# Moving the attention-gate projections of a hybrid attention / SSM layer from the merge into the attention rounds

## The chip, the cores and the metric

The program runs on one core of one Trainium2 chip. The metric is the device time of one execution in microseconds. The kernel before took 1139.73 us (median of 3 runs, 1139.62 to 1141.38).

## The reference

One decoder layer over a sequence of 512 positions with 1024 channels, float32, and a last RMSNorm. Cut to what matters here:

```python
h = rmsnorm(x, norm_mix)
q, c_raw, q_idx, k_idx, w_idx, z, xbc, dt_raw, g_att, g_ssm = split(h @ w_in)
# A: sparse attention, 16 heads over a shared latent, k = 128 keys per query
att   = per-head softmax(q_lat . c_sel * scale + bias) @ c_sel, up-projected by w_uv
y_att = att @ w_att_out
# B: Mamba-2 SSD branch on z, xbc, dt
y_ssm = gated_group_rmsnorm(ssd(...), z) @ w_ssm_out
merged = sigmoid(g_att) * y_att + sigmoid(g_ssm) * y_ssm
x = x + merged @ w_out
h = rmsnorm(x, norm_ffn)
x = x + (silu(gate) * val) @ w_ffn_down      # gate, val: conv3(h @ w_ffn_up)
out = rmsnorm(x, norm_final)
```

g_att and g_ssm are two products of h with 1024 x 1024 pieces of w_in. The kernel writes sigmoid(g) as (tanh(g / 2) + 1) / 2.

## The kernel before

Every matrix product is done in three passes: an operand is split into a rounded high part and the rest (hi, lo), and hi x hi, hi x lo and lo x hi are added up in PSUM (`mm3`, L108; in groups that can be interleaved with other work, `proj_steps`, L373). A projection of 128 output channels over all 512 positions is 24 matmuls of 512 columns. Weights come in tiles of 128 x 1024: `fetch` (L91) loads one into `wr` (2 buffers) through SyncE's queue; `halves` (L101) makes `wh` on ScalarE (L86) and `wl` on GpSimd (L87), 3 buffers each. PSUM has two rings of four tiles, `mm` (projections) and `ch` (all else).

The stages in order: the first norm (`norm_T`, L126, called at L200), which squares and scales four blocks of x (lines L137 to L144), transposes them on TensorE (L146) and splits the result into hTh and hTl (L151, L152), which start in pairs as PSUM comes free; small projections (pkidx, pcr, pqidx); the top-k scores; the SSD branch by four groups; the attention; the merge; the output projection; the FFN; the last norm.

The attention is a loop of 18 rounds (L854). Round h computes the logits of head h (pl, L767, read with the bias and the running maximum by VectorE at L769), softmax (exponentials on ScalarE at L776, reciprocal and four scalings of 128, 256, 384 and 512 columns on VectorE, L778 to L781), the transposes of head h-1's probabilities (pPT, L797), and the product of head h-2's probabilities with V (pav, L816). `weave` (L359) puts fill between these: in even rounds the next query projection (pq, then pk), in odd ones a projection of the SSM gate (pgs, `gs_steps`, L736). Ahead of the rounds stand the first two query projections and the last SSD output projection (pso, L481). The bias rows T are loaded per head (L748).

The merge (L889) does, for each of 8 blocks of 128 channels: the attention-gate projection pga, its tanh (L893), the attention's output projection pao (L896), their product, the sum with the SSM part (L897, L898), and the split into mg.

A framework schedules the written program: it places each instruction on its engine by a model of the engines' times, keeping what depends on what, so the order on an engine differs from the order of the code by small steps. At run time each engine follows its own order and waits at semaphores. SyncE's queue issues the DMAs in its order too: one that waits holds those behind it.

Of the kernel before, what the change touches and what calls it, by code (L numbers as in the profile page):

```python
# [9 lines left out]
F32 = mybir.dt.float32  # L10
R32 = mybir.dt.float32r
AF = mybir.ActivationFunctionType
OP = mybir.AluOpType

P = 128
S = 512
NB = S // P
D = 1024
KD = D // P
# [29 lines left out]
def _body(ctx, tc, x, prm_d, cst_d, nfin_d, wI_d, wX_d, wSO_d, wQ_d, wG_d, wAO_d, wO_d, wUp_d, wDn_d,  # L49
          wkv_d, out):  # L50
    nc = tc.nc
# [10 lines left out]
    def mmt(name):  # L62
        return pm.tile([P, 512], F32, tag="mm", name=name)

    def cht(name):
        return pc.tile([P, 512], F32, tag="ch", name=name)
# [17 lines left out]
    def split(hi, lo, src, lo_eng=None):  # L84

        nc.scalar.activation(hi, src, AF.Copy)  # L86
        (lo_eng or nc.vector).tensor_tensor(lo, src, f(hi), OP.subtract)  # L87
# [10 lines left out]
    def weight(src, w=1024):  # L98
        return halves(fetch(src, w), w)

    def halves(fetched, w=1024):  # L101
        i, raw = fetched
        hi = wp.tile([P, w], R32, tag="wh", name=f"wh{i}", bufs=3)
        lo = wp.tile([P, w], R32, tag="wl", name=f"wl{i}", bufs=3)
        split(hi, lo, raw, lo_eng=nc.gpsimd)
        return hi, lo

    def mm3(ps, terms):  # L108
# [50 lines left out]
    def proj_T(ps, w):  # L159
        mm3(ps, [((w[0][:, k * P:(k + 1) * P], w[1][:, k * P:(k + 1) * P]), actT[k]) for k in range(KD)])  # L160
# [22 lines left out]
    with tc.tile_pool(name="n1", bufs=2) as n1:  # L183
# [13 lines left out]
        w1 = fetch(wI_d[1])  # L197
        nc.sync.dma_start(prm, prm_d)
        nc.sync.dma_start(cs1, cst_d[:, NKEEP:])
        norm_T(xts, "gmix", actT, n1, "vvaa", "aavv")  # L200
        w0, w1 = halves(w0), halves(w1)


        ps = mmt("pkidx")
# [168 lines left out]
    def proj_steps(name, wsrc, after, parts=2):  # L373

        st = {}

        def seq():
            wh, wl = st["w"]
            for a, b in ((wh, 0), (wh, 1), (wl, 0)):
                for k in range(KD):  # L380
                    yield a[:, k * P:(k + 1) * P], actT[k][b]

        def part(j):
            def run():
                if j == 0:
                    st["w"] = weight(wsrc)
                    st["ps"] = mmt(name)
                    st["it"] = list(seq())
                for i in range(24 * j // parts, 24 * (j + 1) // parts):
                    nc.tensor.matmul(st["ps"], *st["it"][i], start=(i == 0), stop=(i == 23))  # L390
                if j == parts - 1:
                    after(st["ps"])
            return run

        return [part(j) for j in range(parts)]
# [320 lines left out]
    def q_steps(p):  # L716
        def after(ps):
            qTs[p] = dup_q(ps, f"qT{p}", ("qh0", "ql0", "qh1", "ql1"), ap_, 0.125, 2)

        def k_step():  # L720
            ps = mmt(f"pk{p}")
            ks = slice(p * P, (p + 1) * P)
            mm3(ps, [((wkv[0][0][:, ks], wkv[0][1][:, ks]), ckvT)])
            kl = ap_.tile([P, S], R32, tag="tmp", name=f"kl{p}", bufs=1)
            kTs[p] = []
            for hh in range(2):
                r, o = slice(64 * hh, 64 * hh + 64), slice(64 - 64 * hh, 128 - 64 * hh)
                kt = ap_.tile([P, S], R32, tag=f"kT{hh}", name=f"kT{p}_{hh}")
                nc.scalar.activation(kt[r], ps[r], AF.Copy)
                nc.vector.tensor_tensor(kl[r], ps[r], f(kt[r]), OP.subtract)  # L730
                nc.sync.dma_start(f(kt[o]), f(kl[r]))
                kTs[p].append(kt)

        return proj_steps(f"pq{p}", wQ_d[p], after, 4) + [k_step]

    def gs_steps(p):  # L736
        def after(ps):
            tg = ap_.tile([P, S], F32, tag="tmp", name=f"tgs{p}", bufs=1)
            nc.scalar.activation(tg, ps, AF.Tanh, scale=0.5)
            nc.vector.scalar_tensor_tensor(yssm[p], tg, 1.0, yssm[p], OP.add, OP.mult)  # L740
        return proj_steps(f"pgs{p}", wG_d[8 + p], after, 4)

    def logits(h):
        p, hh = h // 2, h % 2
        qh, ql = qTs[p][hh]
        kt = kTs[p][hh]
        T = ap_.tile([P, 256], F32, tag="T", name=f"T{h}")
        nc.sync.dma_start(T, bass.AP(tensor=skD.tensor, offset=skD.offset + h * P * UW + 127,  # L748
                                     ap=[[UW - 1, P], [1, 256]]))
        bm = ap_.tile([P, SEGW], F32, tag="bm", name=f"bm{h}", bufs=1)  # L750
        r31 = pv("r31", h, h + 1)
        nc.gpsimd.tensor_tensor(bm[:, 0:P], msk[:, 0:P], T[:, P:], OP.add)
        nc.gpsimd.tensor_tensor(
            bass.AP(tensor=bm.tensor, offset=bm.offset + P, ap=[bm.ap[0], [512, 3], [1, 256]]),
            bass.AP(tensor=msk.tensor, offset=msk.offset + P, ap=[msk.ap[0], [512, 3], [1, 256]]),
            T.unsqueeze(1).to_broadcast([P, 3, 256]), OP.add)
        for i in (2, 3):
            o, n = SEG[i], (i - 1) * P
            nc.gpsimd.tensor_tensor(bm[:, o:o + n], msk[:, o:o + n], r31.to_broadcast([P, n]), OP.add)
        pr = ap_.tile([P, SEGW], F32, tag="pr", name=f"pr{h}")  # L760
        mx = ap_.tile([P, NB], F32, tag="mx", name=f"mx{h}")
        sm = ap_.tile([P, NB], F32, tag="sm", name=f"sm{h}")

        def lg(i):
            o, n = SEG[i], (i + 1) * P
            pl_ = cht(f"pl{h}_{i}")[:, :n]
            nc.tensor.matmul(pl_, qh[:, i * P:(i + 1) * P], kt[:, :n], start=True, stop=False)  # L767
            nc.tensor.matmul(pl_, ql[:, i * P:(i + 1) * P], kt[:, :n], start=False, stop=True)
            nc.vector.tensor_tensor_reduce(pr[:, o:o + n], pl_, bm[:, o:o + n], 1.0, -3e38, OP.add, OP.max,  # L769
                                           mx[:, i:i + 1])  # L770

        def soft():
            nc.vector.tensor_scalar(mx, mx, -1.0, None, OP.mult)  # L773
            for i in range(NB):
                o, n = SEG[i], (i + 1) * P
                nc.scalar.activation(pr[:, o:o + n], pr[:, o:o + n], AF.Exp, bias=mx[:, i:i + 1],  # L776
                                     accum_out=sm[:, i:i + 1])
            nc.vector.reciprocal(sm, sm)  # L778
            for i in range(NB):
                o, n = SEG[i], (i + 1) * P  # L780
                nc.vector.tensor_scalar(pr[:, o:o + n], pr[:, o:o + n], sm[:, i:i + 1], None, OP.mult)  # L781
            prs[h] = pr

        return [lambda i=i: lg(i) for i in range(NB)] + [soft]
# [57 lines left out]
    last_trans()  # L842
    for s_ in qn[1][:-1]:
        s_()
    so[0]()
    so[1]()
    load_kv()
# [3 lines left out]
    so[4]()  # L851
    so[5]()
    qn[1][-1]()
    for h in range(H + 2):  # L854
        p = h // 2
        fl = []
        if h == 2:
            open_att()
        if h < 2:
            hg = len(gs[0]) // 2  # L860
            fl = [so[6 + h]] + gs[0][h * hg:(h + 1) * hg]
        elif h < H:
            if h % 2 == 0 and p + 1 < 8:
                fl = list(qn[p + 1])
            elif h % 2 == 1:
                fl = list(gs[p])
        chain = []
        lg = logits(h) if h < H else []
        chain += [(i < 3, s_) for i, s_ in enumerate(lg[:NB])]
        if h >= 2:  # L870
            chain.append((0, lambda: pav_(h - 2)))
        if 1 <= h <= H:
            chain += [(i == 1, s_) for i, s_ in enumerate(ptrans(h - 1))]
        if h % 4 == 1 and h < H:
            chain.append((0, v_step(h // 4)))
        chain += [(1, s_) for s_ in lg[NB:]]
        if h >= 5 and h % 2 == 1:
            chain.append((0, lambda: att_split((h - 5) // 2)))
        weave(chain, fl)
# [7 lines left out]
    mp = mps.enter_context(tc.tile_pool(name="mp", bufs=1))  # L887
    mg = []
    for d in range(KD):  # L889
        ps = mmt(f"pga{d}")  # L890
        proj_T(ps, weight(wG_d[d]))
        tg = mp.tile([P, S], F32, tag="tg", name=f"tga{d}", bufs=2)
        nc.scalar.activation(tg, ps, AF.Tanh, scale=0.5)  # L893
        ps = cht(f"pao{d}")
        wh, wl = weight(wAO_d[d])
        mm3(ps, [((wh[:, k * P:(k + 1) * P], wl[:, k * P:(k + 1) * P]), attT[k]) for k in range(KD)])  # L896
        nc.vector.scalar_tensor_tensor(tg, tg, 1.0, ps, OP.add, OP.mult)  # L897
        nc.vector.tensor_tensor(tg, tg, yssm[d], OP.add)  # L898
        hi = mp.tile([P, S], R32, tag=f"mh{d}", name=f"mh{d}", bufs=1)
        lo = mp.tile([P, S], R32, tag=f"ml{d}", name=f"ml{d}", bufs=1)  # L900
        split(hi, lo, tg)
        mg.append((hi, lo))
# [207 lines left out]
```

## Time and profile before

| | us |
|---|---|
| median of 3 runs | 1139.73 |
| the profiled execution | 1139.14 |
| its span, first to last instruction | 1137.4 |
| TensorE matmul busy | 1092.4 (96%) |
| VectorE, ScalarE, GpSimd busy | 670.8, 588.5, 504.6 |
| attention, from the first query projection to pao's first | 429 to 637 |
| merge, up to the output projection | 637 to 719 |

The busy time of TensorE is modelled from overlapping matmuls, so the throughput is read from the distance of many matmuls in the chain, and the holes from the time that an engine sat idle before an instruction. Idle time of an engine off the chain costs nothing. The granted clock is a share of 2.4 GHz; the lower of the two levels, 1.2 GHz, is 0.5.

### The profile page before, as it was taken

What the parts mean: (1) busy time and instruction counts of PE and PEld (TensorE: products, weight loads), DVE (VectorE), ACT (ScalarE), POOL (GpSimd) and SP (SyncE); (2) the same over time, 40 slices, a digit from 0 to 9 for tenths busy, and PEclk for the clock granted to TensorE, in tenths of its full rate; (3) what the DMA queues carried; (4) which work ended last, traced back from release to release, by engine and by line L of the source; (5) the groups of instructions that cost most, each with busy time, mean ns of one, the idle gap of its engine ahead of it and who ended that gap; (6) DMA issues with size and microseconds to landing.
All of it is one profiled execution on the core that took longest, in us unless ns stands there. A gap on an engine that the chain in (4) does not pass through costs nothing.

```text
span 1137.4 us, 14581 instructions
## 1 busy us (share of the span) xinstructions
PE 1092.4 (96%) x5268; PEld 908.3 (80%) x5268; DVE 670.8 (59%) x1340; ACT 588.5 (52%) x948; POOL 504.6 (44%) x279
## 2 busy tenths in 40 slices
PE   5999999999999999899998999999999999999997
PEld 5777778788888887787887888878888888888885
DVE  4589999995696894588889433135344343420004
ACT  5364686687777744467666432244444444431223
POOL 3424244345344345656665344443444444444442
PEclk9999999999999999999999999999999999999999
DMA  5464332323332324334433233323322232222322
GB/s 195 117 190 146 111 103 84 105 93 108 102 97 90 130 73 117 127 88 121 130 88 101 86 130 111 112 85 103 109 93 93 97 106 93 93 93 95 106 96 74
DMA packets 43305, 122.06 MB, mean 107 GB/s; under 512 B 5392, under 2 KB 9760, under 8 KB 43232
## 3 DMA queue, kind: packets, MB, share of 16 engines
q1 hardware_dynamic: 42656, 120.07, 33.6%
q10 hardware_dynamic: 576, 1.05, 0.2%
q8 instruction: 42, 0.69, 0.2%
q14 instruction: 31, 0.25, 0.1%
HBM read 108.29 MB, written 5.32 MB: 100 GB/s over the span
## 4 chain that ended last, share of the span: by engine, by line
PE 65%; DVE 19%; ACT 4%; POOL 3%; issue 3%; DMA 1%; POOLq 0%; DVEq 0%; ACTq 0%
PE pup L112 21%; PE pdn L971 10%; PE pxbc L390 6%; PE pso L481 5%; PE pao L112 4%; PE pga L112 4%; PE pwo L915 4%; DVE msk L350 2%; DVE m L349 2%; DVE u L405 2%; DVE pr L781 2%; DVE pr L769 2%; PE pz L456 1%; PE pz L457 1%; PE pz L458 1%
## 5 line engine op out<-in xcount | busy, mean ns | idle before, releaser
L87 POOL TENSOR_TENSOR wl<-wr,wh 128x1024 fp32r<-128x1024 f32 x168 | 406.0, 2417 | 504.3 <-ACT wh L86 250.3
L86 ACT ACTIVATE wh<-wr 128x1024 fp32r<-128x1024 f32 x168 | 177.9, 1060 | 216.7 <-PE pdn L971 80.6
L954 DVE SCALAR_TENSOR_TENSOR fu<-pup,prm,fu 128x511 f32<-128x511 f32 x88 | 65.9, 749 | 124.5 <-ACT fu L952 122.9
L112 PE MATMUL pup<-hTh,wh 128*128 128x512 f32 (+1 forms) x368 | 88.0, 381 | 1.6 <-ACT hTh L151 0.8
L112 PE MATMUL pup<-hTl,wh 128*128 128x512 f32 (+1 forms) x368 | 87.7, 380 | 0.0
L112 PE MATMUL pup<-hTh,wl 128*128 128x512 f32 (+1 forms) x368 | 87.5, 380 | 0.0
L112 PEld LDWEIGHTS pup<-hTh,wh 128*128 128x128 f32 x368 | 67.2, 188 | 15.1 <-ACT hTh L151 1.0
L112 PEld LDWEIGHTS pup<-hTl,wh 128*128 128x128 f32 x368 | 67.3, 188 | 13.1
L112 PEld LDWEIGHTS pup<-hTh,wl 128*128 128x128 f32 x368 | 67.2, 188 | 13.1
L971 PE MATMUL pdn<-wl,fh 128*128 128x512 f32 x176 | 68.6, 390 | 1.2 <-POOL wl L87 1.2
L971 PE MATMUL pdn<-wh,fl 128*128 128x512 f32 x176 | 68.5, 389 | 0.0
L971 PE MATMUL pdn<-wh,fh 128*128 128x512 f32 x176 | 68.4, 390 | 0.0
L998 DVE TENSOR_TENSOR x<-pdn,x 128x512 f32<-128x512 f32 x8 | 5.5, 689 | 104.6 <-PE pdn L971 104.6
L405 DVE SCALAR_TENSOR_TENSOR u<-pxbc,prm,u 128x511 f32<-128x511 f32 (+2 forms) x72 | 53.3, 740 | 8.5 <-ACT u L403 8.3
L456 PE MATMUL pz<-wh,hTh 128*128 128x512 f32 x128 | 51.8, 405 | 1.1 <-DVE u L405 1.1
L390 PE MATMUL pxbc<-hTl,wh 128*128 128x512 f32 x192 | 52.0, 393 | 0.0
L390 PE MATMUL pxbc<-hTh,wh 128*128 128x512 f32 x192 | 51.4, 395 | 0.0
L457 PE MATMUL pz<-wl,hTh 128*128 128x512 f32 x128 | 50.8, 396 | 0.0
L458 PE MATMUL pz<-wh,hTl 128*128 128x512 f32 x128 | 50.7, 396 | 0.0
L390 PE MATMUL pxbc<-hTh,wl 128*128 128x512 f32 x192 | 50.4, 392 | 0.0
L952 ACT ACTIVATE fu<-pup,prm 128x512 f32<-128x512 f32 x44 | 34.3, 780 | 27.4 <-PE pup L112 27.4
L776 ACT ACTIVATE pr<-pr,mx 128x128 f32<-128x128 f32 (+1 forms) x64 | 35.5, 556 | 14.5 <-DVE mx L773 14.5
(361 smaller groups left out, 2514.2 us busy)
## 6 DMA issues: line engine op xcount, KB each, us to landing
wr<-wUp SPq DMA_DIRECT2D x44, 512.0 KB, 3.5
wr<-wX SPq DMA_DIRECT2D x40, 512.0 KB, 3.5
wr<-wDn SPq DMA_DIRECT2D x22, 512.0 KB, 3.4
dec<-acD SPq DMA_DIRECT2D x32, 256.0 KB, 3.8
wr<-wSO SPq DMA_DIRECT2D x16, 512.0 KB, 3.5
wr<-wG SPq DMA_DIRECT2D x16, 512.0 KB, 3.7
x<-x SPq DMA_DIRECT2D x8, 512.0 KB, 4.5
wr<-wQ SPq DMA_DIRECT2D x8, 512.0 KB, 3.5
```

What stands on the lines that cost most here:

```text
L86: nc.scalar.activation(hi, src, AF.Copy)
L87: (lo_eng or nc.vector).tensor_tensor(lo, src, f(hi), OP.subtract)
L112: nc.tensor.matmul(ps, l, r, start=(i == 0), stop=(i == len(seq) - 1))
L390: nc.tensor.matmul(st["ps"], *st["it"][i], start=(i == 0), stop=(i == 23))
L405: nc.vector.scalar_tensor_tensor(u[:, d:], ps[:, :S - d], pv("cw", o + 3 - d, o + 4 - d), u[:, d:], OP.mult, OP.add)
L456: nc.tensor.matmul(ps, actT[k][0][:, bs], wh[:, ws], start=(k == 0), stop=False)
L457: nc.tensor.matmul(ps, actT[k][0][:, bs], wl[:, ws], start=False, stop=False)
L458: nc.tensor.matmul(ps, actT[k][1][:, bs], wh[:, ws], start=False, stop=(k == KD - 1))
L481: nc.tensor.matmul(ps, *seq[i], start=(i == 0), stop=(i == 11))
L915: nc.tensor.matmul(po8[b][hf], l[:, bs], r[:, ws], start=(k == 0 and i == 0), stop=(k == KD - 1 and i == 2))
L954: nc.vector.scalar_tensor_tensor(u[:, d:], ps[:, :S - d], pv("fw", o + 2 - d, o + 3 - d), u[:, d:], OP.mult, OP.add)
L971: nc.tensor.matmul(po8[b][hf], l[:, bs], r[:, ws], start=(k == 0 and i == 0), stop=(k == NF - 1 and i == 2))
```

## The change

Four things change.

The attention-gate projections (pga) leave the merge. `ga_steps(d)` builds each as four groups of six matmuls, like those of pgs; their tanh is written to a DRAM tile gaD. The first of the eight runs ahead of pso, the other 28 groups are dealt to the 18 rounds by `GA_SHARE` and mixed into each round's fill. The merge loads the tanh back (tile tg, four buffers), and its pao takes PSUM tiles from both rings in turn.

The tile kl / tgs / tga has two buffers instead of one, and the bias rows T have one instead of two.

The scalings of 384 and 512 probabilities go from VectorE to ScalarE.

In the first norm, ScalarE squares three blocks (before: two) and scales none; VectorE squares one and scales all four. The wl of the first weight tile (w0) goes from GpSimd to VectorE.

```diff
+TMP = 2
+GA_SHARE = (1, 1, 1, 1, 1, 1, 1, 1, 1, 1, 1, 1, 1, 1, 3, 1, 2, 2)
...
-        norm_T(xts, "gmix", actT, n1, "vvaa", "aavv")
-        w0, w1 = halves(w0), halves(w1)
+        norm_T(xts, "gmix", actT, n1, "vaaa", "vvvv")
+        w0, w1 = halves(w0, lo_eng=nc.vector), halves(w1)
...
-            kl = ap_.tile([P, S], R32, tag="tmp", name=f"kl{p}", bufs=1)
+            kl = ap_.tile([P, S], R32, tag="tmp", name=f"kl{p}", bufs=TMP)
...
+    gaD = dram.tile([KD, P, S], F32, tag="gaD", name="gaD")
+
+    def ga_steps(d):
+
+        def after(ps):
+            tg = ap_.tile([P, S], F32, tag="tmp", name=f"tga{d}", bufs=TMP)
+            nc.scalar.activation(tg, ps, AF.Tanh, scale=0.5)
+            nc.sync.dma_start(gaD[d], tg)
+        return proj_steps(f"pga{d}", wG_d[d], after, 4)
...
-        T = ap_.tile([P, 256], F32, tag="T", name=f"T{h}")
+        T = ap_.tile([P, 256], F32, tag="T", name=f"T{h}", bufs=1)
...
-                nc.vector.tensor_scalar(pr[:, o:o + n], pr[:, o:o + n], sm[:, i:i + 1], None, OP.mult)
+                if i < 2:
+                    nc.vector.tensor_scalar(pr[:, o:o + n], pr[:, o:o + n], sm[:, i:i + 1], None, OP.mult)
+                else:
+                    nc.scalar.activation(pr[:, o:o + n], pr[:, o:o + n], AF.Copy, scale=sm[:, i:i + 1])
...
+    gas = [s_ for d in range(KD) for s_ in ga_steps(d)]
+    for s_ in gas[:4]:
+        s_()
     so[0]()
     so[1]()
...
+        want = 4 + (32 - 4) * sum(GA_SHARE[:h + 1]) // sum(GA_SHARE)
+        new = gas[gdone:want]
+        gdone = want
+        fl = [s_ for _, s_ in sorted([((i + 0.5) / max(len(fl), 1), s_) for i, s_ in enumerate(fl)]
+                                     + [((i + 0.4) / max(len(new), 1), s_) for i, s_ in enumerate(new)],
+                                     key=lambda t: t[0])]
...
-        ps = mmt(f"pga{d}")
-        proj_T(ps, weight(wG_d[d]))
-        tg = mp.tile([P, S], F32, tag="tg", name=f"tga{d}", bufs=2)
-        nc.scalar.activation(tg, ps, AF.Tanh, scale=0.5)
-        ps = cht(f"pao{d}")
+        tg = mp.tile([P, S], F32, tag="tg", name=f"tg{d}", bufs=4)
+        nc.sync.dma_start(tg, gaD[d])
+        ps = (cht if d % 2 else mmt)(f"pao{d}")
```

How the order moves at the three places of which the prediction speaks. First GpSimd in the first norm: nrsgmix are the four reciprocal roots of the norm, wl the subtractions of weight tiles; here the rows before

```order
L118 TENSOR_TENSOR nrsgmix_142<-rsq,mhalf 128x1
L118 TENSOR_TENSOR nrsgmix_158<-rsq,mhalf 128x1
L87 TENSOR_TENSOR wl_241<-wr_128,wh_240 128x1024
L118 TENSOR_TENSOR nrsgmix_194<-rsq,mhalf 128x1
L118 TENSOR_TENSOR nrsgmix_210<-rsq,mhalf 128x1
L87 TENSOR_TENSOR wl_245<-wr_132,wh_244 128x1024
```

and the rows now:

```order
L120 TENSOR_TENSOR nrsgmix_142<-rsq,mhalf 128x1
L120 TENSOR_TENSOR nrsgmix_158<-rsq,mhalf 128x1
L120 TENSOR_TENSOR nrsgmix_194<-rsq,mhalf 128x1
L120 TENSOR_TENSOR nrsgmix_210<-rsq,mhalf 128x1
L89 TENSOR_TENSOR wl_245<-wr_132,wh_244 128x1024
```

The first subtraction has gone to VectorE, between the scalings of x1 and x2; the second stands behind the last root as before, but its wh is now made on ScalarE ahead of the hTh copies, where it stood among them.

Then ScalarE in round 0 and the beginning of round 1 (exponentials L776, weight copies L86, copies of transposed probabilities PTh L800), before

```order
L776 ACTIVATE pr_4565,sm_4567<-pr_4565,mx_4566 128x384
L776 ACTIVATE pr_4565,sm_4567<-pr_4565,mx_4566 128x512
L86 ACTIVATE wh_4902<-wr_4900 128x1024
L800 ACTIVATE PTh_4643<-pPT_0_4675 128x512
L800 ACTIVATE PTh_4643<-pPT_1_4682 128x512
```

and now (L788 the exponentials, L796 the scalings):

```order
L788 ACTIVATE pr_4600,sm_4602<-pr_4600,mx_4601 128x384
L788 ACTIVATE pr_4600,sm_4602<-pr_4600,mx_4601 128x512
L796 ACTIVATE pr_4600<-pr_4600,sm_4602 128x384
L796 ACTIVATE pr_4600<-pr_4600,sm_4602 128x512
L88 ACTIVATE wh_4826<-wr_4824 128x1024
L815 ACTIVATE PTh_4691<-pPT_0_4729 128x512
L815 ACTIVATE PTh_4691<-pPT_1_4736 128x512
```

The two long scalings follow the exponentials directly here; in later rounds a weight copy stands between.

Last TensorE in round 14, from the third logits to pav, before

```order
L767 MATMUL pl_2_6220<-kT_0_6067,qT7h_6035 128x384
L768 MATMUL pl_2_6220<-kT_0_6067,qT7l_6036 128x384
L767 MATMUL pl_3_6224<-kT_0_6067,qT7h_6035 128x512
L768 MATMUL pl_3_6224<-kT_0_6067,qT7l_6036 128x512
L390 MATMUL pgs_6296<-hTh_76,wh_6292 128x512
L390 MATMUL pgs_6296<-hTh_78,wh_6292 128x512
L390 MATMUL pgs_6296<-hTh_80,wh_6292 128x512
L390 MATMUL pgs_6296<-hTh_82,wh_6292 128x512
L816 MATMUL pav_6228<-PTh_6085,V_6159 128x512
```

and now:

```order
L779 MATMUL pl_2_6410<-kT_0_6238,qT7h_6221 128x384
L780 MATMUL pl_2_6410<-kT_0_6238,qT7l_6222 128x384
L392 MATMUL pga_6295<-hTl_85,wh_6291 128x512
L392 MATMUL pga_6295<-hTl_87,wh_6291 128x512
L392 MATMUL pga_6295<-hTl_89,wh_6291 128x512
L392 MATMUL pga_6295<-hTl_91,wh_6291 128x512
L392 MATMUL pga_6295<-hTh_76,wl_6292 128x512
L392 MATMUL pga_6295<-hTh_78,wl_6292 128x512
L779 MATMUL pl_3_6420<-kT_0_6238,qT7h_6221 128x512
L780 MATMUL pl_3_6420<-kT_0_6238,qT7l_6222 128x512
L831 MATMUL pav_6424<-PTh_6256,V_6343 128x512
```

Before, the round had no projection of its own, and the schedule drew four matmuls of the next round's pgs forward; now a group of six pga matmuls stands between the logits, and another between the second and the third.

## Rows read from the trace of the kernel before

**Rows 1.** The page: the chain by line, and the costliest weight groups.

```profile
PE pup L112 21%; PE pdn L971 10%; PE pxbc L390 6%; PE pso L481 5%; PE pao L112 4%; PE pga L112 4%; PE pwo L915 4%; DVE msk L350 2%; DVE m L349 2%; DVE u L405 2%; DVE pr L781 2%; DVE pr L769 2%; PE pz L456 1%; PE pz L457 1%; PE pz L458 1%
...
L87 POOL TENSOR_TENSOR wl<-wr,wh 128x1024 fp32r<-128x1024 f32 x168 | 406.0, 2417 | 504.3 <-ACT wh L86 250.3
L86 ACT ACTIVATE wh<-wr 128x1024 fp32r<-128x1024 f32 x168 | 177.9, 1060 | 216.7 <-PE pdn L971 80.6
```

**Rows 2.** Busy time by stretch, attention and merge: length, five engines, clock, DMA.

```profile
422.00:452.00 30.00, 27.77 (x137) 22.56 (x135) 15.80 (x29) 14.24 (x23) 16.51 (x11) 1.00 0.42 114
452.00:468.00 16.00, 14.64 (x66) 11.69 (x65) 4.75 (x10) 6.02 (x7) 10.15 (x5) 1.00 0.48 156
468.00:484.00 16.00, 13.59 (x65) 11.04 (x64) 12.19 (x26) 7.15 (x18) 8.71 (x9) 0.89 0.32 94
484.00:610.00 126.00, 123.00 (x664) 103.43 (x663) 108.42 (x255) 86.20 (x204) 81.11 (x71) 1.00 0.41 113
610.00:633.00 23.00, 19.42 (x109) 15.47 (x108) 20.98 (x49) 14.08 (x34) 10.18 (x8) 1.00 0.14 41
633.00:719.00 86.00, 86.00 (x380) 70.89 (x380) 28.98 (x24) 26.99 (x33) 36.19 (x15) 1.00 0.35 118
```

**Rows 3.** The chain in the merge (start, length, what), and the tanh there.

```profile
642.82 5.44 PE pga L112 x24
...
L893 ACT ACTIVATE tga<-pga x8: 597/597/602, 640.5 to 713.6; 128x512 f32<-128x512 f32 x8
```

**Rows 4.** TensorE in time order: start, length, idle before and its releaser.

```profile
450.15 1.19 PE L481 MATMUL pso<-yTh,wh 128*128 128x512 f32 x4 [1.73 <-ACT wh L86]
...
452.62 1.20 PE L481 MATMUL pso<-yTh,wl 128*128 128x512 f32 x4 [0.36 <-POOL wl L87]
...
478.36 1.73 PE L797 MATMUL pPT<-cst,pr 128*128 128x128 f32 x6 [2.17 <-DVE pr L781]
479.74 2.06 PE L390 MATMUL pgs<-hTl,wh 128*128 128x512 f32 x4
...
616.15 0.82 PE L816 MATMUL pav<-PTh,V 128*128 128x512 f32 x4 [2.69 <-DVE mx L769]
```

**Rows 5.** VectorE's scalings and GpSimd's subtractions beside them, in time order.

```profile
475.12 3.58 DVE L781 TENSOR_SCALAR pr<-pr,sm 128x128 f32<-128x128 f32 x4
...
475.75 2.34 POOL L87 TENSOR_TENSOR wl<-wr,wh 128x1024 fp32r<-128x1024 f32 x1 [0.29 <-ACT wh L86]
...
611.65 3.54 DVE L781 TENSOR_SCALAR pr<-pr,sm 128x384 f32<-128x384 f32 x2
...
627.79 1.28 DVE L781 TENSOR_SCALAR pr<-pr,sm 128x128 f32<-128x128 f32 x4
```

**Rows 6.** Groups by shape, 484 to 630 us; ScalarE, 420 to 640; DMA landings.

```profile
L781 DVE TENSOR_SCALAR pr<-pr,sm 128x512 f32<-128x512 f32 x15 | 13.7, 916 | 0.0
...
L781 DVE TENSOR_SCALAR pr<-pr,sm 128x384 f32<-128x384 f32 x15 | 7.9, 526 | 0.0
...
L625 ACT ACTIVATE zs<-zs,urs 128x512 f32<-128x512 f32 x4 | 2.6, 712 | 2.5 <-POOL urs L118 2.5
...
wr<-wG SPq DMA_DIRECT2D x16, 512.0 KB, 3.7
...
T<-skD SPq DMA_DIRECT2D x10, 128.0 KB, 2.1
```

**Rows 7.** The first norm in time order, ScalarE, VectorE, GpSimd, TensorE.

```profile
9.88 2.17 ACT L142 ACTIVATE xngmix<-x,nrsgmix 128x1024 f32<-128x1024 f32 x2
...
15.50 0.75 DVE L144 TENSOR_SCALAR xngmix<-x,nrsgmix 128x1024 f32<-128x1024 f32 x1 [0.67 <-POOL nrsgmix L118]
16.17 3.22 DVE L152 SCALAR_TENSOR_TENSOR hTl<-nTgmix,prm,hTh 128x256 fp32r<-128x256 f32 x8
...
16.59 2.37 POOL L87 TENSOR_TENSOR wl<-wr,wh 128x1024 fp32r<-128x1024 f32 x1 [1.13 <-ACT wh L86]
...
18.27 0.98 PE L112 MATMUL pkidx<-hTh,wh 128*128 128x256 f32 x6 [0.87 <-DVE hTl L152]
```

More of the change, by code (lines that the diff above doesn't have):

```diff
@@ L99, in weight, with halves @@
         return halves(fetch(src, w), w)
-    def halves(fetched, w=1024):
+    def halves(fetched, w=1024, lo_eng=nc.gpsimd):
         i, raw = fetched
@@ L104, in halves @@
         lo = wp.tile([P, w], R32, tag="wl", name=f"wl{i}", bufs=3)
-        split(hi, lo, raw, lo_eng=nc.gpsimd)
+        split(hi, lo, raw, lo_eng=lo_eng)
         return hi, lo
@@ L737, in after @@
         def after(ps):
-            tg = ap_.tile([P, S], F32, tag="tmp", name=f"tgs{p}", bufs=1)
+            tg = ap_.tile([P, S], F32, tag="tmp", name=f"tgs{p}", bufs=TMP)
             nc.scalar.activation(tg, ps, AF.Tanh, scale=0.5)
@@ L853, in _body @@
     qn[1][-1]()
+    gdone = 4
     for h in range(H + 2):
```

## Prediction

> **What bounds the kernel now.** I read the chain of waits first, then busy time by stage, then the gaps of TensorE in time order, then who held the engine that TensorE waited for. In the chain the reader is to see that nearly all of it is matmul lines: pga and pao, the two that the merge interleaves, hold 4% each [rows 1]. In the table by stage the merge (633 to 719 us) has TensorE busy for all of its 86.00 us, and the chain there holds 24 pga matmuls in 5.44 us at a time, 0.227 us per matmul, in turn with as many pao matmuls in as long, without a gap [rows 2, 3]. So the merge is bound by TensorE's throughput. The attention before it (422 to 633) is bound by TensorE too, but with holes. TensorE's busy time falls short of the five stretches by 2.23, 1.36, 2.41, 3.00 and 3.58 us, 12.6 us in all [rows 2]. In the third stretch the granted clock is 0.89 on average; 0.11 of 16 us is 1.8 us of work lost to the lower of the two levels, right after the longest hole of that stretch: four pgs matmuls behind it took 2.06 us [rows 4], where six run in 1.36 us at full rate. Together the holes are worth 14.4 us.
>
> Three holes make most of it. At 450.15 and 452.62 pso waits 1.73 and 0.36 us for a weight tile. At 478.36 the transposes of the first probabilities wait 2.17 us for VectorE's scalings. At 616.15 pav waits 2.69 us for a PSUM tile that VectorE has yet to read [rows 4]. Behind the last two stands one thing: four scalings of a head took 1.28 us at 627.79, but 3.58 us at 475.12, and the two long ones alone 3.54 us at 611.65; in the slow cases GpSimd ran a 2.3 us weight subtraction in the middle, and VectorE went on only when it was over [rows 5].
>
> **The change part by part.**
>
> Merge: it loses eight pga projections, 8 x 5.44 = 43.5 us of a stretch without holes [rows 3]. The eight tanh (0.597 us each [rows 3]) leave ScalarE, which was not the bound there. In their place stand eight 256 KB loads. The trace has no load of this tile; the nearest rows are 128 KB in 2.1 us and 512 KB in 3.7 us [rows 6], so I take 3 us, against 5.44 us per pao and four buffers: nothing on the path. The last one is the tightest: its tanh, store and load have to end before the first pao's sum is added, but all loads wait behind that store on SyncE's queue. Tanh 0.6, store 3, load 3 make 6.6 us from the end of pga, 1.2 us later than pao's 5.44; the sum only frees PSUM tiles and TensorE has eight of them, so I cost it at nothing (1.2 us if the cover were gone). Weight tiles still come one per 5.44 us, against 2.42 us of GpSimd for one [rows 1]. Attention's last tile pair keeps its cover, since the last pga now runs just where the first ran before.
>
> Attention: it gains the same 192 matmuls, 43.5 us, of which what falls into holes is free. Four groups run before pso; the other 28 groups of six (1.36 us each) are spread over the 18 rounds: one or two a round, two or three in the last two, and four in round 14, which had no projection of its own.
> (a) Ahead of pso now stand 5.44 us of pga. One more weight tile goes through GpSimd first (2.42 us), but the wait of 1.73 + 0.36 us is covered by the remaining 3 us: 2.1 us won.
> (b) Round 1: the long scalings follow the exponentials on ScalarE. The only ScalarE row of that width from SBUF to SBUF with a scale is 0.71 us [rows 6], so 384 and 512 columns cost about 0.55 + 0.71 = 1.3 us a head. They replace 0.53 + 0.92 = 1.44 us on VectorE [rows 6] and cannot be held up as the VectorE ones were. With two more pga groups (2.7 us) ahead of the transposes, the 2.17 us wait and the stretch at the lower clock go; I take 4.0 of 2.41 + 1.8 us.
> (c) Rounds 2 to 13 (484 to 610): the holes are 126.00 - 123.00 = 3.0 us [rows 2]. They are short waits for a PSUM tile; pga now stands between two logits, and VectorE is relieved. I take half, 1.5 us.
> (d) Round 14: 3.58 us in the stretch, of which 2.69 us is one wait. Two pga groups ahead of pav (2.7 us) and the shorter VectorE queue remove it; I take 3.0 us.
> What is late next in (b) to (d) is the exponentials, which read the last logits' maximum; ScalarE is busy 86.2 of 126 us there [rows 2], and gains 1.3 us for each of 12 heads plus some four weight tiles with a tanh (1.7 us each), so 109 of about 145 us: not a bound.
> The second buffer for kl, tgs and tga costs nothing. T loses one of its two buffers: its load now waits for the head before it, as its load for two heads later did. It lands in 2.1 us [rows 6], and about 9 us pass from head to head.
>
> First norm. ScalarE no longer scales x0 and x1 (2.17 us [rows 7]), so the squares of x2 and x3 can start when their data lands. The first tiles are transposed earlier, but nothing waits for that: the first pkidx matmul at 18.27 waits for hTl on VectorE, and the hTl start right behind the scaling of x3, which took 0.75 us from 15.50 [rows 7]. That scaling moves up by at most the 1.5 us between the two squares and the work before them. Against it: the subtraction wl that ran at 16.59 now follows on GpSimd directly behind the last root, for which the scaling of x3 waits too; if its wh is made by then, the scaling starts second and waits out 2.37 us, as the probabilities did at 611.65 [rows 5, 7]. With both 2.37 us and the 1.5 us, 0.9 us are lost; the hTl for which pkidx waits is now the fourth and not the fifth, 3.22 / 8 = 0.4 us less [rows 7]. Bounds: 1.9 us won, 0.9 us lost. No row tells the two starts apart; wh now has its place ahead of the hTh copies, so I take the lost race: 0.5 us lost.
> The Trainium skill ("SBUF — State Buffer", section "SBUF: two separate sides") says that VectorE and GpSimd share one port pair as an exclusive lock, that whoever starts first holds it for a whole instruction, and that TensorE and ScalarE never wait for it. By that rule the start loses its race and the long scalings on ScalarE keep their time. The rows agree as far as they go: 1.28 us free, 3.58 us beside a subtraction [rows 5].
>
> Sum, against the profiled execution's 1139.14 us (span 1137.4): 43.5 - 43.5 - 2.1 - 4.0 - 1.5 - 3.0 + 0.5 = -10.1, so **1129.0 us**. The median of the runs is 0.6 us above that execution, which I leave aside.
>
> **Rivals.**
> 1. The holes stay: each is a chain of latencies on VectorE, ScalarE and GpSimd that runs after the fill just as it ran before. For it: rounds 2 to 13 had fill and kept 3.0 us. Against: the two largest holes follow VectorE's long scalings, which leave. Time: 1139.1 + 0.5 = 1139.6.
> 2. Weight tiles become the bound: two projections now run in turns through three buffers of wh and wl, where one did. A tile that finds no buffer comes 1.06 us (wh) to 3.7 + 1.06 = 4.8 us (fetch and wh) late [rows 1, 6], for eight more tiles. With wh and wl behind it (3.5 us each) this is 28 us: 1129.0 + 28 = 1157. It decides from 10.1 / 8 = 1.3 us per tile on. For it: at 450.15 TensorE did wait for wh. Against: between 484 and 610 there are only 3.0 us of holes with 12 tiles fetched, and GpSimd is busy 81.1 of 126 us [rows 2].
> 3. Half of it: the fill helps at 450 and in round 14, but ScalarE's queue, with the scalings behind a weight copy of 1.06 us, hands the probabilities over late, by a third of a copy in each of 16 rounds, 5.6 us: 1134.6. For it: the order of those rounds. Against: the fill lengthens each round by 1.7 us.
> 4. All holes go and the first norm wins its race: 1139.1 - 14.4 - 1.9 = 1122.8. For it: 43.5 us of fill against 14.4 us of holes. Against: not every hole has fill in front of it.
>
> **How the numbers follow.** Forecast 0.55 (own range 1126 to 1132), rival 3 0.20, rival 4 0.09, rival 1 0.09, rival 2 0.07. A measurement of this kernel can tell 0.2%, about 2.3 us, from no change. Rival 1 is the same, rival 2 slower, the others faster: 0.84, 0.09, 0.07. The range 1123 to 1137.5 holds the forecast, rivals 3 and 4 but for their edges, and leaves out 1 and 2.
>
> **What would show it.** In the profile after, the merge should be eight pao groups of 5.44 us with no hole; no granted clock under 1.00 near the first rounds of attention; no wait of pPT for VectorE scalings; no wait of 2.7 us in round 14. At the start, a scaling of x3 of over 2 us on VectorE shows the lost race, and 0.75 us shows it won. TensorE waits on wh or wl lines in the rounds would show rival 2; waits for pr on ScalarE rival 3. The prediction is wrong if attention grows by more than 38 us while the merge shrinks by 43.5.

## The result, and the profile after

The changed kernel took 1128.62 us (median of 4 runs, 1125.10 to 1129.59), 0.9892 of the kernel before on the same chip (95% interval 0.9873 to 0.9910); the two medians alone, 1128.62 and 1139.73, give 0.990, inside that interval. The forecast was 1129.0 us. Its profiled execution is the fastest of the four, 1125.1 us with a span of 1123.1 us; against the profiled execution of before that is 14.0 us less, where the sum of the prediction had 10.1. Part of what follows is about these 4 us.

By the first matmul of each step, the span splits in three:

| stretch | before | after | difference |
|---|---|---|---|
| start to the first query projection | 429.19 | 426.95 | -2.24 |
| attention and merge: from there to the output projection | 289.62 | 277.65 | -11.97 |
| from there to the end of the span | 418.54 | 418.52 | -0.02 |

The middle stretch is a clean comparison: both kernels run the same 1368 matmuls in it, 952 of them 512 columns wide. What can differ is the holes, the clock, and how closely the matmuls follow each other.

The merge in the chain of waits of the changed kernel (start, length, what):

```profile
660.90 43.85 PE pao L114 x192
704.76 40.13 PE pwo L938 x177
```

Eight pao blocks run in one piece, 5.48 us each, where pga and pao took turns at 5.44 [rows 3]. Nothing waits there.

Busy time by stretch after (columns as in [rows 2]: length, the five engines' busy time, granted clock, DMA):

```profile
452.00:468.00 16.00, 13.63 (x62) 10.96 (x61) 5.36 (x10) 5.07 (x7) 8.77 (x4) 1.00 0.59 188
468.00:484.00 16.00, 16.00 (x87) 13.74 (x86) 8.88 (x25) 8.26 (x22) 7.97 (x8) 1.00 0.22 67
484.00:634.00 150.00, 147.09 (x782) 125.18 (x781) 103.49 (x243) 108.41 (x239) 95.48 (x79) 1.00 0.42 118
661.00:704.70 43.70, 43.70 (x193) 35.78 (x192) 27.41 (x23) 13.49 (x17) 19.44 (x8) 1.00 0.54 187
```

The stretch 468 to 484 had a hole and a clock of 0.89 before [rows 2]; it now has neither. The hole at 452 to 468 is new in size. What TensorE waited for, from the attention to the end of the merge (total us, times, longest):

```profile
PE pl L779 <- DMA kT<-kl: 2.4, 1, 2.4
PE pV L114 <- DVE cr L838: 2.2, 3, 0.9
PE pPT L812 <- DVE mx L781: 0.7, 1, 0.7
PE pyT L633 <- ACT zs L627: 0.5, 2, 0.3
PE pPT L812 <- ACT pr L796: 0.3, 1, 0.3
```

The waits of [rows 4] for a weight tile, for VectorE's scalings and for the PSUM tile ahead of pav are gone. The largest one left is the first logits' wait for a copy of kT. TensorE's idle time in the stretch is 6.1 us in all, where the prediction read 12.6 before, and the low clock that it priced at 1.8 us is gone: 8.3 of the 12.0 us. The other 3.7 us stand in no row. The ends of matmuls are modelled, so a hole can cost more than the idle time that the view shows.

The first norm, VectorE, GpSimd and then ScalarE in time order (start, length, idle before and its releaser):

```profile
13.15 0.75 DVE L146 TENSOR_SCALAR xngmix<-x,nrsgmix 128x1024 f32<-128x1024 f32 x1 [0.66 <-POOL nrsgmix L120]
...
12.56 0.55 POOL L120 TENSOR_TENSOR nrsgmix<-rsq,mhalf 128x1 f32<-128x1 f32 x1 [0.93 <-DVE rsq L119]
13.33 2.80 POOL L89 TENSOR_TENSOR wl<-wr,wh 128x1024 fp32r<-128x1024 f32 x1 [0.22 <-ACT wh L88]
...
12.20 1.06 ACT L88 ACTIVATE wh<-wr 128x1024 fp32r<-128x1024 f32 x1
```

The scaling of x3 began at 13.15 us (15.50 before [rows 7]) and took 0.75 us: the race that the prediction gave up was won, by 0.18 us. The subtraction, first in GpSimd's queue behind the root, still waited 0.22 us for its wh, which ended at 13.26. The first pkidx matmul moved from 18.27 to 15.53 us, and the small projections end 2.2 us earlier.

### The profile page after: what moved, and what is told of

The parts are those of the page before. It is cut to its first block, busy times and chain, and to the rows that moved or that the text cites. A ratio compares the mean times of both kernels' runs of the same rounds, so it can differ in the third digit from the quotient of the medians.

```text
span 1123.1 us, 14582 instructions
## 1 busy us (share of the span) xinstructions
PE 1087.0 (97%) x5268; PEld 906.1 (81%) x5268; DVE 656.2 (58%) x1309; ACT 603.6 (54%) x980; POOL 502.9 (45%) x278
## 4 chain that ended last, share of the span: by engine, by line
PE 70%; DVE 17%; ACT 4%; POOL 2%; DMA 2%; issue 1%; POOLq 0%; ACTq 0%; DVEq 0%
PE pup L114 21%; PE pdn L994 10%; PE pxbc L392 6%; PE pao L114 4%; PE pso L483 4%; PE pwo L938 4%; PE pga L392 3%; PE pgs L392 3%; PE pq L392 2%; DVE msk L352 2%; DVE m L351 2%; DVE u L407 2%; PE pz L459 1%; PE pz L458 1%; PE pz L460 1%
## 5 line engine op out<-in xcount | busy, mean ns | idle before, releaser
L788 ACT ACTIVATE pr<-pr,mx 128x128 f32<-128x128 f32 (+1 forms) x64 | 35.5, 558 | 33.4 <-DVE mx L785 33.3
```

## The experiments

The length of the attention and merge stretch is read from each kernel's trace in the same way, always over the same 1368 matmuls. Low clock says where in it a granted clock under 1.00 was seen.

| kernel | median us | ratio to before (interval) | attention and merge | low clock in it |
|---|---|---|---|---|
| before | 1139.7 to 1141.2 | 1 | 289.62 | 478 |
| changed | 1128.62 | 0.9892 (0.9873 to 0.9910) | 277.65 | none |
| e1 norm back | 1131.02 | 0.9905 (0.9880 to 0.9931) | 279.38 | 470 |
| e2 norm late | 1130.58 | 0.9911 (0.9889 to 0.9933) | 277.96 | none |
| e3 scalings back | 1137.88 | 0.9979 (0.9962 to 0.9996) | 288.54 | 467 |
| e4 scalings alone | 1143.20 | 1.0023 (1.0008 to 1.0038) | 291.81 | 564, 609 |
| e5 none ahead | 1128.21 | 0.9895 (0.9870 to 0.9921) | 279.47 | 450 |
| e6 kT queue | 1123.27 | 0.9849 (0.9820 to 0.9877) | 275.84 | none |
| e7 one buffer | 1129.54 | 0.9908 (0.9874 to 0.9942) | 279.49 | 466 |
| e8 negation | 1124.74 | 0.9860 (0.9831 to 0.9889) | 275.71 | 469 |
| e9 scalings and negation | 1131.05 | 0.9919 (0.9892 to 0.9946) | 282.02 | none |
| e10 kT queue and negation | 1121.67 | 0.9831 (0.9813 to 0.9848) | 271.79 | none |

**The first norm put back (e1).**

```diff
-        norm_T(xts, "gmix", actT, n1, "vaaa", "vvvv")
-        w0, w1 = halves(w0, lo_eng=nc.vector), halves(w1)
+        norm_T(xts, "gmix", actT, n1, "vvaa", "aavv")
+        w0, w1 = halves(w0), halves(w1)
```

> The changed kernel with the first norm's order put back as it was before (two squares and two scalings on each of VectorE and ScalarE, the first weight tile's subtraction on GpSimd). Theory, from the trace of the changed kernel: the new order won its race there, x3's scaling began at 13.15 us against 15.50 before, and the small projections ended 2.2 us earlier; so this kernel is 2.2 us slower than the changed one, about 8.8 us faster than before (ratio to before 0.992). Rival, the prediction on record: the new order costs 0.5 us, so this kernel is 0.5 us faster than the changed one. Second rival: the 2.2 us were luck of that one execution, and the two agree within 0.5 us.

Measured: the transposes that follow the small projections (pw) start at 29.77 us, 27.79 in the changed kernel and 29.98 before: 2.0 us of the 2.2 are the norm's order. The other traces agree. With the old order pw starts at 29.47 (e4) and 29.54 us (e9). With the new one it starts at 27.67 to 28.02 us in e3, e5, e6, e7 and e10, and at 29.01 in e8, where the first square on ScalarE started 0.6 us later than in the changed kernel. The scaling of x3 takes 0.75 us in all seven traces with the new order as it stands, with a lead of 0.17 to 0.24 us. The whole time moved by 2.4 us in the medians, with intervals that overlap. By the traces the new order is a gain of about 2 us, and not a loss.

**The last root delayed (e2).** Two tiny operations on VectorE delay the last root; the order of every engine is otherwise the same.

```diff
         nc.vector.tensor_scalar(t, ss, scale, eps, OP.mult, OP.add)
+        for _ in range(late):
+            nc.vector.tensor_scalar(t, t, 1.0, 0.0, OP.mult, OP.add)
...
-                rsqrt(rs, ss, 1.0 / D, EPS, 1, pool)
+                rsqrt(rs, ss, 1.0 / D, EPS, 1, pool, 2 if gname == "gmix" and b == 3 else 0)
```

> The changed kernel with two more VectorE operations of 128x1 (0.15 us each, multiply by one) ahead of the last root of the first norm; nothing else moves on any engine. Theory: the scaling of x3 began 0.18 us ahead of GpSimd's subtraction in the changed kernel; 0.3 us of delay lets the subtraction start first, and the scaling then stands for the 2.4 us of it: the scaling's row reads over 2 us, the first projection starts about 2.4 us later, and the kernel is 2.0 to 2.7 us slower than the changed one. Rival, no lock between the two engines (or a shared one): the scaling still takes 0.75 us, and the kernel is 0.3 us slower.

Its trace, VectorE and then GpSimd, columns as above:

```profile
12.56 0.34 DVE L121 TENSOR_SCALAR rsq<-rsq 128x1 f32<-128x1 f32 x2
13.56 2.83 DVE L148 TENSOR_SCALAR xngmix<-x,nrsgmix 128x1024 f32<-128x1024 f32 x1 [0.66 <-POOL nrsgmix L122]
...
12.98 0.55 POOL L122 TENSOR_TENSOR nrsgmix<-rsq,mhalf 128x1 f32<-128x1 f32 x1 [1.30 <-DVE rsq L121]
13.50 2.34 POOL L89 TENSOR_TENSOR wl<-wr,wh 128x1024 fp32r<-128x1024 f32 x1
```

0.34 us of work turned 0.75 us into 2.83: the subtraction began 0.06 us ahead and the scaling stood until it was over. pkidx started at 18.07 us (15.53 in the changed kernel), 2.5 us later where about 2.4 was expected. pw came 3.9 us later, at 31.68. The median is 2.0 us higher, with 2.0 to 2.7 expected and intervals that overlap. The rule that the prediction cited from the Trainium skill ("SBUF — State Buffer", section "SBUF: two separate sides"), that whoever starts first keeps the port pair for its whole instruction (the section names the VectorE operations for which it holds), agrees with this trace. What failed was the reading of who starts first.

**The scalings back on VectorE (e3), and alone (e4).** e3 is the changed kernel with the one line of before for all four scalings; e4 is the kernel before with

```diff
-                nc.vector.tensor_scalar(pr[:, o:o + n], pr[:, o:o + n], sm[:, i:i + 1], None, OP.mult)
+                if i < 2:
+                    nc.vector.tensor_scalar(pr[:, o:o + n], pr[:, o:o + n], sm[:, i:i + 1], None, OP.mult)
+                else:
+                    nc.scalar.activation(pr[:, o:o + n], pr[:, o:o + n], AF.Copy, scale=sm[:, i:i + 1])
```

> The changed kernel with all four scalings of the probabilities on VectorE, as before; TensorE's order stays. Theory A, the fill alone covers the holes: round 1 has two pga groups (2.7 us) ahead of the transposes against the 2.2 us wait of before, round 14 has two against 2.7 us; the kernel is 0 to 1.5 us slower than the changed one, and no granted clock of 0.5 appears near the first rounds. Theory B, the holes went because the long scalings left VectorE: the waits of 2.2 us in round 1 and 2.7 us in round 14 come back in some part, with the low clock behind the first, and the kernel is 4 to 7 us slower than the changed one.

> The kernel before with the long scalings on ScalarE, and nothing else of the change. Theory A (the fill covers the holes): without it the chain logits, maximum, exponentials, scalings, transposes stays as long but for VectorE's stalls; this kernel gains 1 to 3 us on before. Theory B (VectorE's scalings were the cause): both holes and the low clock behind the first go without any fill, 5 to 7 us faster than before (ratio 0.994 to 0.996).

Both theories fell. The fill alone wins 1.1 us of the stretch (288.54), the scalings alone lose 2.2 (291.81), both together win 12.0. Of the 2.2 us, a second spell of low clock (1.7 us, as worked out from e8 below) is a part. The medians agree in sign: 1140.58 us for the kernel before in these runs, 1137.88 for e3, which has the new norm too, and 1143.20 for e4. In e3 the hole of round 1 is still filled, but TensorE waits elsewhere:

```profile
PE pl L779 <- DVE V L714: 2.8, 2, 2.1
PE pV L114 <- DVE cr L835: 2.6, 3, 0.9
PE pav L828 <- DVE mx L781: 2.3, 3, 1.3
PE pPT L809 <- DVE pr L793: 2.1, 1, 2.1
PE pl L779 <- DMA kT<-kl: 1.8, 1, 1.8
PE pPT L809 <- DVE mx L781: 1.4, 4, 0.7
```

All but the kT line end on VectorE, and 15 of its 64 scalings take over 1 us (11 before): more weight tiles per round mean more subtractions to stand behind. Three of them as one row, and GpSimd's rows of the same time:

```profile
535.60 5.25 DVE L793 TENSOR_SCALAR pr<-pr,sm 128x256 f32<-128x256 f32 x3
...
535.49 1.29 POOL L841 TENSOR_TENSOR cr<-cr,atl 128x512 f32<-128x512 f32 x1 [2.13 <-DMA atl<-ath]
536.74 2.45 POOL L89 TENSOR_TENSOR wl<-wr,wh 128x1024 fp32r<-128x1024 f32 x1
```

In e4 only one scaling still takes that long. What stands now is a smaller operation on the same path, the negation of the maxima (128x4), for which the exponentials wait (start, length, idle before; GpSimd, VectorE, ScalarE, TensorE):

```profile
517.21 1.84 POOL L753 TENSOR_TENSOR bm<-msk,T 128x768 f32<-128x768 f32 x1
517.49 1.58 DVE L773 TENSOR_SCALAR mx<-mx 128x4 f32<-128x4 f32 x1
...
519.11 0.40 ACT L776 ACTIVATE pr<-pr,mx 128x128 f32<-128x128 f32 x1 [2.37 <-DVE mx L773]
...
521.00 0.38 PE L112 MATMUL pV<-uvh,ckh 128*128 128x256 f32 x1 [2.31 <-DVE cr L826]
```

This happens to seven of 16 negations, 1.57 to 2.38 us each. ScalarE's queue is late by that much, and with it ScalarE's copy of one half of pav; VectorE's copy of the other half (cr), which frees the PSUM tile for pV, waited 1.18 us for it.

**The negation moved too (e9 and e8).** e9 is e4, and e8 the changed kernel, with

```diff
-            nc.vector.tensor_scalar(mx, mx, -1.0, None, OP.mult)
+            nc.scalar.activation(mx, mx, AF.Copy, scale=-1.0)
```

> The kernel before with the long scalings on ScalarE and the negation of the maxima on ScalarE too. With the scalings alone moved, seven of 16 negations took 1.6 to 2.4 us on VectorE (0.17 us free), since they now met GpSimd's bias additions. Theory: that is where the gain of the scalings went, about 1.5 us a time on the way to the exponentials; with the negation moved as well this kernel gains 3 to 6 us on the one with the scalings alone and is 3 to 6 us faster than before. Rival: without fill the chain of the softmax is as long whatever engine negates: within 1 us of the scalings alone.

> The changed kernel with the negation of the maxima (mx, 128x4, 16 of them) on ScalarE and not on VectorE; TensorE's and GpSimd's orders stay. In the changed kernel four of 16 stood 1.1 to 2.4 us behind GpSimd's work and the exponentials waited. Theory: these stalls reach TensorE only where the fill ahead of pV and pPT runs out, in the rounds at 528, 576, 621 and 624 us (0.8 to 1.1 us each): 1 to 3 us faster. Rival: the holes come from PSUM (pV waits until VectorE has copied pav to cr), whatever the negation does: within 0.7 us.

The negation's row in e4 (minimum, median, maximum in ns):

```profile
L773 DVE TENSOR_SCALAR mx<-mx x16: 170/415/2380, 471.4 to 624.0; 128x4 f32<-128x4 f32 x16
```

and in e9:

```profile
L773 ACT ACTIVATE mx<-mx x16: 188/205/217, 476.1 to 619.4; 128x4 f32<-128x4 f32 x16
```

The stretch goes from 291.81 to 282.02 us, more than the 3 to 6 expected: 16 operations of 0.2 us were worth 9.8 us, of which two spells of low clock are a part (3.4 us). Here is where the gain of the scalings had gone. The negation moved by itself, with the scalings left on VectorE, was not run; in the kernel before only one of its 16 took over 1 us (1.23).

e9 moves no projection, and yet its stretch is 7.6 us shorter than before (3 to 6 expected), and the interval of its ratio overlaps that of the changed kernel. So what the move of the projections is worth depends on the softmax beside it: 1.1 us with all of it as before (e3), 14.2 with the long scalings on ScalarE (e4 to the changed kernel), 6.3 with the negation there too (e9 to e8).

On top of the fill (e8) the rounds lose their holes too, 3.4 us between the first pav and that of head 12, a little over the expected 1 to 3; but the wait for kT stands, and this time the clock fell behind it.

**The first kT (e6), and both (e10).**

```diff
-                nc.sync.dma_start(f(kt[o]), f(kl[r]))
+                (nc.scalar if p == 0 else nc.sync).dma_start(f(kt[o]), f(kl[r]))
```

> The changed kernel with the two copies of the first kT issued from ScalarE's queue and not from SyncE's, where they stand behind a weight load that waits for its buffer until 461.0 us. Theory: kT waits for its place in the queue; the first logits start 1.5 to 2.4 us earlier, the wait of 2.4 us on kT shrinks under 1 us, and the kernel is 1.5 to 2.4 us faster than the changed one by the trace. Rival: the transfer itself (4.7 us from issue to landing beside a 512 KB load) or the subtraction kl is what is late: under 0.7 us won.

In the changed kernel the two copies stand behind a weight load on SyncE, which waits for its buffer (issues, then TensorE's first logits):

```profile
461.00 0.33 SPq L97 DMA_DIRECT2D wr<-wQ  x1
461.42 1.10 SPq L733 DMA_DIRECT2D kT<-kl  x2
...
466.28 0.30 PE L779 MATMUL pl<-kT,qT0h 128*128 128x128 f32 x1 [2.37 <-DMA kT<-kl]
```

From ScalarE's queue in e6:

```profile
460.11 0.52 ACTq L733 DMA_DIRECT2D kT<-kl  x1
...
463.52 0.22 PE L779 MATMUL pl<-kT,qT0h 128*128 128x128 f32 x1
```

The copy is issued 1.3 us earlier, ahead of the 512 KB load and not beside it. It lands 2.7 us after its issue and not 4.7, so that 2.0 of the 3.3 us by which it lands earlier are the transfer's, which the rival held for the cause, and 1.3 the queue's. The edit changes both at once, and which of them was needed is not shown. The wait is gone. The stretch is 1.8 us shorter, 2.65 up to the first pav; 0.8 comes back in small waits of the rounds. The median fell by more, to 1123.27, and the four runs lie within 0.7 us, where those of the changed kernel lie within 4.5.

> The changed kernel with both edits that won: the copies of the first kT on ScalarE's queue, and the negation of the maxima on ScalarE. Theory (the two holes are independent, one before the first logits, one in the rounds): from the first query projection to the output projection 277.6 us in the changed kernel, 275.8 with the queue, and without the holes at 528, 576 and 621 to 624 (3.4 us by the trace of the negation alone) 272.4 us; no low clock near 469 us; 1119.5 to 1121.5 us in all (ratio to before 0.981 to 0.984). Rival: the holes hand their time on to the next wait, and the two together win no more than the better one: 1122.5 to 1124.

271.79 us against 272.4 expected: the two holes are independent. The median, 1121.67 us, is 0.2 us over the range of 1119.5 to 1121.5 and clear of the rival's 1122.5 to 1124; the ratio is inside its own range. What TensorE waits for in the whole of attention and merge is now

```profile
PE pyT L633 <- ACT zs L627: 0.5, 2, 0.3
PE pPT L812 <- ACT pr L796: 0.3, 1, 0.3
PE pV L114 <- DVE cr L838: 0.2, 1, 0.2
```

At 1121.67 us this version is 1.7% under the kernel before, and its interval lies clear of the changed kernel's, though not of e6's.

**No projection ahead of pso (e5).** The four groups `gas[:4]` are left to the rounds.

> The changed kernel with no pga ahead of pso: all 32 groups are dealt to the rounds by the same shares. Theory (the 5.44 us ahead of pso cover its weight waits): the waits of pso for wh and wl come back with about 2.1 us, while the wait of the first logits for kT, 2.4 us in the changed kernel and 1.0 us before, shrinks to about 1 us; the kernel is 0 to 1.5 us slower than the changed one. Rival: the place of these 24 matmuls is worth nothing, since a wait before the first logits takes over what is won ahead of pso: equal within 0.5 us by the holes of the trace, and the waits of both kinds add up to the same. Second rival: more fill in the rounds closes holes there too, 1 us faster.

pso waited for wh again, and the logits waited less, with a low clock behind pso's wait:

```profile
PE pso L483 <- ACT wh L88: 2.0, 1, 2.0
...
PE pl L779 <- issue: 0.4, 1, 0.4
```

The two make 2.4 us, as long as the one wait for kT in the changed kernel, and all listed waits of the stretch make 6.2 us against 6.1. So the rival holds: by the waits the place of these 24 matmuls is worth nothing, since the logits' wait takes over what is won ahead of pso. The stretch is 1.8 us longer, and the spell of low clock is 1.7 us of that. The medians differ by 0.4 us.

**One buffer (e7).** `TMP = 1`.

> The changed kernel with one buffer, and not two, for kl, tgs and tga. Theory (the prediction's: the second buffer costs nothing and is worth little): tanh of pga then waits until the store of the last one has landed (about 2 to 3 us after its issue) or the product of the last tgs is done, but with one or two projections per round of about 11 us that is hidden: within 0.7 us of the changed kernel. Rival: the subtraction kl and with it kT stand behind a store in SyncE's queue, the logits wait at each new pair of heads (8 times up to 1.5 us) and the low clock follows: 4 to 12 us slower.

The rounds differ from the changed kernel's by under 0.4 us each, and no wait on kl or tga appears; what is longer is the place of the kT wait (2.0 us here), behind which the clock fell. The rival is out, and a cost under 1 us can't be excluded.

## Why the prediction was right, and where it was not

The change of the attention and merge stretch, less the added wide matmuls at 0.2267 us [rows 3], step by step:

| step | length before | after | wide matmuls added | difference | forecast |
|---|---|---|---|---|---|
| (a), (b): to the first pav | 61.47 | 63.59 | 36 | -6.0 | -6.1 |
| (c): to pav of head 11 | 111.79 | 129.21 | 90 | -3.0 | -1.5 |
| (d): to pav of head 12 | 13.70 | 12.63 | 8 | -2.9 | -3.0 |
| the rest, with the merge | 102.66 | 72.21 | -134 | -0.1 | 0 |
| first norm | | | | -2.2 | +0.5 |

**The merge** was right: the rest of the stretch comes out within 0.1 us. 43.5 us moved at their full price, because there was no hole to lose. The load of tg landed in 3.3 us (median of 8) and the store in 3.0, 3 each in the working, with the cover that it named.

**(a) and (b)** have the right sum from a partly wrong account. pso's waits went, 2.1 us, and come back in e5. But the first logits' wait grew from 1.0 to 2.4 us, and the sum had no term for it: (a) kept 0.7 us, and by e5 nothing. kT's copy stood behind the same weight load before:

```profile
459.79 0.33 SPq L95 DMA_DIRECT2D wr<-wQ  x1
460.21 0.47 SPq L731 DMA_DIRECT2D kT<-kl  x1
...
464.40 0.30 PE L767 MATMUL pl<-kT,qT0h 128*128 128x128 f32 x1 [1.00 <-issue]
```

In the changed kernel the copy is issued 1.2 us later and takes 4.7 us to land and not 4.1, while TensorE reaches the logits only 0.5 us later, at 463.91 for 463.40. Round 1 won its 4.0, 2.4 us of waits and the clock, and 1.3 us more by difference that no row accounts for: no idle time is left between 468 and 484 us. The fill is enough for that, since e3 keeps it with the scalings on VectorE; the scalings are enough too, since e4 without the fill is 3.9 us shorter than before up to the first pav.

**(c) and (d)** have the right mechanism and a wrong share. The prediction let fill and VectorE's relief each do some of it. e3 shows that with the fill alone (c) is 3.4 us longer than before, and not 3.0 shorter, because the fill brings more subtractions for VectorE's scalings to stand behind. e4 shows that the relief alone makes (c) 5.0 us longer, with 1.7 us of low clock in it, since the negation stands in their place. In the changed kernel four negations still stood 1.1 to 2.4 us, but with a projection ahead of each consumer only 3.4 us of that reached TensorE (e8, e10). (c) was also sized too small: half of 3.0 us, by choice and not from a row. TensorE's idle time there did fall by about half, from 2.7 to 1.3 us, but the length fell by 3.0 us. The sum took idle time for the price of a hole, and here that is too little: the prediction put all holes of the stretch and their clock at 14.4 us, and e10 won 17.8 us of it.

**The first norm** is the step that failed: "so I take the lost race: 0.5 us lost" against 2.2 us won, outside the stated bound of 1.9. Two things were wrong. The scaling of x3 moved up by 2.35 us and not "by at most the 1.5 us": the squares of x2 and x3 on ScalarE no longer stand behind 2.17 us of scalings. And wh was not "made by then": with three squares and two weight copies on it, ScalarE finished wh at 13.26 us, after the root at 13.11. The race turns on 0.2 us, as e2 shows, and it went the same way in all seven traces of this order; but no row of before could tell that, so both outcomes should have stood in the sum with their prices.

**The rivals.** Rival 1 comes out by its size in e3, with the softmax as before: 1.1 us won in the stretch, though by other holes than those of before. Weight tiles did not become the bound: no row of TensorE's waits in the rounds names wh or wl. ScalarE's queue cost 0.3 us, once; the two long scalings took 0.72 and 0.61 us, 1.33 a head where 1.3 was taken. The profiled execution, 1125.1 us, lies between the forecast and rival 4 (1122.8), and rival 4's condition, that all holes go, is what e10 brought about but for 1.0 us, at 1121.7.

**Why the median still met the forecast.** In part by luck: two errors of about 4 us cancel. The sum was 4 us too cautious for the profiled execution (2.7 in the norm, 1.4 in the holes), and the median lies 3.5 us above that execution, which the sum had not counted. The other three runs of the changed kernel took 2.9 to 4.5 us longer, at a mean clock of 0.994 to 0.996 against 0.997. On 1126 us, 0.001 to 0.003 of the clock are 1.1 to 3.4 us of work, so the clock explains a part of this; that it explains all is not shown, and these runs have no trace that tells where it fell. In the attention and merge the traces show one place of the changed kernel where the clock can fall: behind the wait for kT. Granted clock (the column before the last two) from 464 to 476 us, in the changed kernel:

```profile
464.00:476.00 12.00, 9.72 (x47) 8.27 (x48) 4.36 (x14) 2.87 (x9) 3.77 (x3) 1.00 0.31 88
```

in e8, with the same wait:

```profile
464.00:476.00 12.00, 9.97 (x40) 7.93 (x39) 4.44 (x11) 2.24 (x3) 2.37 (x2) 0.86 0.47 137
```

and in e6, without it:

```profile
464.00:476.00 12.00, 12.00 (x58) 10.12 (x57) 6.61 (x21) 5.08 (x13) 5.35 (x5) 1.00 0.30 96
```

In e8 TensorE ran at the lower level for part of the stretch, 0.14 x 12 = 1.7 us of work, behind a hole of 2.0 us. Six traces have this wait with 1.8 to 2.4 us: in e1, e3, e7 and e8 the clock fell behind it, in the changed kernel and e2 it did not. Without the wait (e6) the trace is 2.0 us shorter and the median 5.3 us lower, which fits low clocks behind it in the untraced runs.

Ahead of the attention the clock falls in other places, behind holes that neither kernel was meant to change. TensorE has a hole of 1.5 us ahead of pckv near 45 us in all twelve traces, and the clock fell behind it in six, the changed kernel among them. A hole of 1.33 us ahead of py near 150 us is in eleven, and the clock fell there in five, not in the changed kernel. The kernel before reached its first query projection at 429.19 us, and e9, the same program up to there, at 433.60; the clock fell at 48 and 120 us in the one, at 57 and for longer at 152 us in the other. No experiment was aimed at this, and it stays open.

## What to carry to other kernels

Work that is moved into holes is paid for by the holes only if what makes them does not grow with it: here each projection that filled a hole brought a GpSimd subtraction that could hold VectorE. When an operation is taken off a contended engine, look at what the same path still has there; here a 0.17 us negation, left behind, turned a gain of 7.6 us into a loss of 2.2. What a hole costs is read from the length of a stretch with and without it, since the idle time shown gave 8.3 us with the clock where 12.0 were won. And of a race that turns on a few tenths of a microsecond, write both outcomes with their prices rather than one.

## What the runs showed of the hardware that was not expected

The price of a lost start does not follow the size of the operation that loses it: 128x4 negations took 1.57 to 2.38 us in e4 (0.17 free), until the GpSimd operation beside them was over. The reciprocals of the same 128x4 on the same engine took 0.17 to 0.18 us in all twelve traces, although 5 to 14 of their 16 ran wholly inside a GpSimd operation. A hole of 1.8 to 2.4 us on TensorE was followed by the low clock in four of six traces, one of 1.5 us in six of twelve and one of 1.33 us in five of eleven, so one profile of such a kernel shows only one of its outcomes. Without the wait for kT four runs lay within 0.7 us (e6) and within 2.2 us (e10), where those of the changed kernel lie within 4.5.
